# Turning branch B's queries and keys with DMA transposes instead of TensorE, in a streaming encoder step on one Trainium2 core

## The chip, the cores and the metric

The kernel runs on one core of one Trainium2 chip. The metric is the device time of one execution in microseconds (us); the time of the kernel before is the median of three runs. Beside the runs there is one profiled execution, from which every row of the trace comes.

## What is computed

One layer of a streaming encoder. A prompt of 2048 tokens and eight running streams of 16 new tokens each go through the same weights. The layer is normalised and modulated, projected by one wide matrix, mixed by two attention branches side by side, gated, merged and projected back. Cut to what matters here:

```python
h, gate = adaln_modulate(x, c, norm_g, w_ada, b_ada)
qa, ka, va, za, qb, kb, vb, zb, ga, gb = project_inputs(h, w_in, pos)   # d_model 1024

# branch A: 4 heads of 2 x 64, two softmaxes, one subtracted from the other
s = einsum('bqhcd,bkhcd->bhcqk', qa, ka) * 64 ** -0.5
p = softmax(where(mask, s, -inf)); w = p[:, :, 0] - lam * p[:, :, 1]
oa = einsum('bhqk,bkhe->bqhe', w, va)

# branch B: 8 heads of 64, stick breaking: a running product from the last key to the first
z = einsum('bqhd,bkhd->bhqk', qb, kb) * 64 ** -0.5
log_1m = where(mask, log_sigmoid(-z), 0)
a = where(mask, exp(log_sigmoid(z) + cumsum(log_1m, reverse=True) - log_1m), 0)
ob = einsum('bhqk,bkhd->bqhd', a, vb)

y = (sigmoid(ga) * ((rms(oa) * silu(za)) @ w_a) + sigmoid(gb) * ((ob * silu(zb)) @ w_b)) @ w_out
```

The outputs are the layer's rows and the new keys and values of both branches, all in float32.

## The kernel before

Products on TensorE are done in float16 with each number split into a high and a low half: high by high, high by low and low by high are added up. `q16` and `k16` are such pairs of halves for a tile of 128 tokens, with the tokens on the partitions. For the scores TensorE needs them turned, with the head's 64 numbers (and the two halves) on the partitions: these turned tiles are called `qst` (4 blocks of 128 x 128) and `k` (2 blocks).

**Units and tiles.** The middle of the kernel, from about 130 to about 1840 us, runs over 8 units. Even units are one head of branch A, odd units (`kind` 1) two heads of branch B. A unit has 17 tiles of 128 tokens: first the one of the eight streams (`t == NT`, kept as `sam` and stored for later), then 16 of the prompt. For every tile there are these steps:

- `project` (line 438): 24 products into PSUM bank `mm`; then ScalarE and VectorE write `pr` (float32 for the outputs), the values `vt`, the keys `k16` (line 304) and the queries `q16` (lines 472 and 473; one of two buffers `qbuf`). In odd units 24 more products (line 514) make gate columns in PSUM bank `t`, and ScalarE evacuates them (line 517, `gt`).
- `transpose_qk`: turns `k16` and `q16` into `k` and `qst`. It is put behind the sixth piece of the next tile's projection. Before the change six products with an identity matrix (lines 527 and 531) write into bank `t`, of which there is one buffer, and two copies (lines 541 and 542) take them to SBUF: ScalarE's in branch A, VectorE's in branch B.
- `scores` (lines 649 and 650): products of `qst` and `k`, in chunks of 512 keys; then in branch A a softmax on VectorE and ScalarE, in branch B two sigmoids on ScalarE, a scan on VectorE (line 626) and a product on GpSimd (line 632). The weights are split into halves (lines 582 and 583, or 299 and 304) and turned by a DMA from SBUF to SBUF (`turn`, line 590) into `wt`.
- `pv` (lines 706 to 711): products of `wt` with the values, two jobs later (`PV_LAG`).

**Order.** Projections run ahead of the scores by `LEAD` tiles at the start, and are spread evenly over the time; `interleave` mixes the pieces of projection, scores and `pv` in Python, and a scheduler that estimates when each instruction can begin then sets the final order on each engine. Between these pieces the weights of the next unit and the caches of the running streams are loaded and split. After the units come the cached attention of the eight streams, the merge and the output projection.

**Queue.** Nearly all DMAs are issued by SyncE (SP), one after another in the order of its program: `load` is `nc.sync.dma_start`, and the transposes of line 590 are `nc.sync.dma_start_transpose`. Among them are `hs` (line 415, the normalised input of a tile's projection), the stores of `pr` (lines 494, 495), `gt` (line 518) and `o` (line 700).

Of the kernel before, what the change touches and what calls it, by code (L numbers as in the profile page):

```python
# [17 lines left out]
F16 = mybir.dt.float16  # L18
# [7 lines left out]
P = 128  # L26
# [87 lines left out]
def layer_kernel(ctx: ExitStack, tc: tile.TileContext, a: dict):  # L114
    nc = tc.nc
    V, S, G, T = nc.vector, nc.scalar, nc.gpsimd, nc.tensor
# [79 lines left out]
    def bank(tag, dt=F32):  # L196
        return ps.tile([P, 512 if dt == F32 else 1024], dt, tag=tag, name=f"ps_{tag}", bufs=BANKS[tag])
# [5 lines left out]
    id16 = con.tile([P, P], F16, name="id16")  # L203
# [318 lines left out]
    def transpose_qk(U, t):  # L522
        g, i = t // 4, t % 4
        q16, k16 = U.pop(("q16", t)), U.pop(("k16", t))
        pt = bank("t", F16)
        for c in range(2):
            T.transpose(pt[:, c * P : (c + 1) * P], k16[:, c, :, :].rearrange("p f d -> p (f d)"), id16)
        for f in range(2):
            for c in range(2):
                j = 2 + f * 2 + c  # L530
                T.transpose(pt[:, j * P : (j + 1) * P], q16[:, f, c, :, :].rearrange("p r d -> p (r d)"), id16)
        if t == NT:
            sam = stg.tile([P, 6, P], F16, tag="sam", name="sam", bufs=1)
            qst, kst = sam[:, 0:4, :], sam[:, 4:6, :]
        else:
            if i == 0:
                U["k"][g] = kvp.tile([P, 2, 512], F16, tag="k", name="k", bufs=K_BUFS)
            U["q", t] = qst = stg.tile([P, 4, P], F16, tag="qst", name="qst", bufs=Q_BUFS)
            kst = U["k"][g][:, :, i * P : (i + 1) * P]
        copy = V.tensor_copy if U["kind"] == 1 else S.copy  # L540
        copy(out=kst, in_=pt[:, 0:256].rearrange("p (c n) -> p c n", c=2))
        copy(out=qst, in_=pt[:, 256:768].rearrange("p (j n) -> p j n", j=4))  # L542
        if t == NT:
            load(out=s_d[U["u"]][:, 0:6, :], in_=sam)

# [374 lines left out]
    for m in range(len(steps)):  # L920
        starts.append(len(line))
        for i, fn in enumerate(projection(m)):
            line.append((m, fn))
            if i == TR_AFTER and m > 0:
                line.append((m - 1, lambda m=m: transpose_qk(units[steps[m - 1][0]], steps[m - 1][1])))
    line.append((len(steps) - 1, lambda: transpose_qk(units[7], NT - 1)))
    starts.append(len(line))
    at = [0]
# [27 lines left out]
    with tc.tile_pool(name="p0", bufs=1) as p0:  # L956
# [34 lines left out]
        pt = bank("t")  # L991
# [33 lines left out]
        pt = bank("t")  # L1025
# [266 lines left out]
    for n in range(len(steps) + PV_LAG):  # L1292
        made, qk, vs = [], [], []
        if n < len(steps):
            u, t = steps[n]
# [184 lines left out]
```

## Time and profile before

| | |
|---|---|
| runs of the kernel before | 2333.37, 2330.89, 2333.27 us; median 2333.27 us |
| the profiled execution | 2326.12 us, of which the span of its instructions is 2324.3 us |
| mean granted TensorE clock | 0.969 |
| HBM read, written | 228.82 MB, 86.02 MB |

The span is the time from the first to the last instruction. A row of the busy table gives an engine's busy time, its share of the span and its count of instructions; PE is TensorE's products and PEld its weight loads. A busy time of PE is not work at its peak: products are pipelined, and each record holds its whole way through the array. DMA share is the mean busy share of the core's 16 DMA engines.

### The profile page before, as it was taken

How to read it: one execution, taken by the hardware profiler on the slowest of the kernel's cores; microseconds unless marked ns; L12 is line 12 of the kernel's file. 1: busy time of each engine (PE TensorE's matmuls, PEld its weight loads, DVE VectorE, ACT ScalarE, POOL GpSimd, SP SyncE). 2: the span in 40 equal slices, each digit the busy share in tenths (PEclk: the TensorE clock that was granted, in tenths of full speed). 3: DMA queues.
4: the chain of work that ended last, by engine and by line, in shares of the span. 5: the costliest groups of instructions: out<-in, count | busy, mean ns of one | idle time of the engine just before them, and what ended most of it. 6: DMA issues, size and time to landing. Idle time of an engine off the chain costs nothing. (4 is left out here: it accounts for less than half of the span.)

```text
span 2324.3 us, 41797 instructions
## 1 busy us (share of the span) xinstructions
PE 2096.5 (90%) x14752; PEld 1123.2 (48%) x14752; DVE 1745.0 (75%) x3795; ACT 1621.7 (70%) x3228; POOL 704.5 (30%) x610
## 2 busy tenths in 40 slices
PE   5998899998989889899998998999998689899998
PEld 3654454444545445455554444555454344444443
DVE  4658668789776777997767879787778878777763
ACT  4968676788776677878676887776677666556541
POOL 1223014356410433752023346401345312122111
PEclk7999999999999999999999999999999799999999
DMA  9778558889696798878877898665667899778421
GB/s 335 272 213 212 134 146 220 198 198 184 174 239 150 201 231 186 187 184 220 183 200 206 182 221 199 171 156 138 142 157 165 191 273 256 211 219 215 143 100 52
DMA packets 805827, 445.30 MB, mean 192 GB/s; under 512 B 537354, under 2 KB 744506, under 8 KB 805104
## 3 DMA queue, kind: packets, MB, share of 16 engines
q1 hardware_dynamic: 804668, 442.24, 76.4%
q8 instruction: 115, 1.88, 0.3%
q14 instruction: 96, 0.79, 0.1%
q10 hardware_dynamic: 948, 0.39, 0.1%
HBM read 228.82 MB, written 86.02 MB: 135 GB/s over the span
## 5 line engine op out<-in xcount | busy, mean ns | idle before, releaser
L632 POOL TENSOR_TENSOR sc_p<-sc_p,sc_n 128x127 f32<-128x127 f32 (+7 forms) x192 | 311.8, 1628 | 660.2 <-DVE sc_n L626 562.8
L438 PEld LDWEIGHTS <-hs 128*128 128x128 f16 x3120 | 276.5, 99 | 263.3 <-issue 11.9
L438 PE MATMUL ps_mm<-wa,hs 128*128 128x512 f16 x1590 | 400.4, 382 | 2.9 <-DMA hs<-hT_d 2.1
L438 PE MATMUL ps_mm<-wb,hs 128*128 128x512 f16 x1530 | 394.5, 384 | 7.6 <-DMA hs<-hT_d 6.8
L626 DVE TENSOR_TENSOR_SCAN sc_n<-ps_s,sc_n,zero_t 128x512 f32<-128x512 f32 x192 | 245.4, 1278 | 72.2 <-ACT ps_s L123 67.3
L649 PE MATMUL ps_s<-k,qst 128*128 128x512 f16 (+3 forms) x640 | 226.0, 354 | 49.2 <-DVE sc_n L626 38.5
L583 DVE TENSOR_TENSOR sc_n<-sc_p,sc_n 128x128 f16<-128x128 f32 (+7 forms) x192 | 222.7, 1163 | 36.8 <-ACT sc_n L582 36.4
L514 PEld LDWEIGHTS <-hs 128*128 128x128 f16 x1632 | 156.5, 98 | 189.1 <-ACT qst L542 5.9
L123 ACT ACTIVATE sc_p<-ps_s,usc 128x512 f32<-128x512 f32 (+3 forms) x320 | 205.1, 641 | 32.5 <-PE ps_s L650 23.3
L650 PE MATMUL ps_s<-k,qst 128*128 128x512 f16 (+3 forms) x640 | 225.7, 354 | 0.0
L514 PE MATMUL ps_t<-wb,hs 128*128 128x512 f16 x918 | 216.1, 379 | 3.0 <-DVE sam L542 1.4
L710 PE MATMUL ps_o<-v,wt 128*128 128x128 f16 x1088 | 168.9, 225 | 43.1 <-DMA wt<-sc_n 42.7
L123 ACT ACTIVATE ps_s<-ps_s,usc 128x512 f32<-128x512 f32 (+3 forms) x328 | 200.5, 611 | 0.0
L582 ACT CAST sc_n<-sc_p 128x128 f16<-128x128 f32 (+7 forms) x192 | 155.2, 811 | 63.7 <-POOL sc_p L632 62.8
L1395 PE MATMUL ps_o<-wo,wb 128*128 128x512 f16 x816 | 185.2, 382 | 6.3 <-ACT wo L299 5.5
L514 PE MATMUL ps_t<-wa,hs 128*128 128x512 f16 x714 | 170.6, 381 | 6.9 <-ACT qst L542 5.7
L710 PEld LDWEIGHTS <-wt 128*128 128x128 f16 x1088 | 105.0, 101 | 104.7 <-DMA wt<-sc_n 54.6
L711 PE MATMUL ps_o<-v,wt 128*128 128x64 f16 x1088 | 154.5, 198 | 0.0
L568 DVE TENSOR_SCALAR_CACHE_REDUCE sc_n<-ps_s,usc 128x512 f32<-128x512 f32 (+3 forms) x160 | 106.2, 664 | 35.2 <-PE ps_s L650 17.2
L1366 PEld LDWEIGHTS <-wb 128*128 128x128 f16 x816 | 79.2, 100 | 105.5 <-issue 23.1
L711 PEld LDWEIGHTS <-wt 128*128 128x128 f16 x1088 | 102.9, 100 | 50.9 <-issue 2.2
L1395 PEld LDWEIGHTS <-wb 128*128 128x128 f16 x816 | 78.7, 98 | 100.4 <-issue 9.1
(370 smaller groups left out, 4515.6 us busy)
## 6 DMA issues: line engine op xcount, KB each, us to landing
hs<-hT_d SPq DMA_DIRECT2D x130, 512.0 KB, 4.6
g_d<-gt SPq DMA_DIRECT2D x68, 256.0 KB, 4.3
out_dram<-pr SPq DMA_DIRECT2D x204, 64.0 KB, 2.2
wa<-g_d SPq DMA_DIRECT2D x25, 512.0 KB, 3.8
o_d<-o SPq DMA_DIRECT2D x136, 64.0 KB, 2.6
hs<-o_d SPq DMA_DIRECT2D x17, 512.0 KB, 3.8
out_dram<-x SPq DMA_DIRECT2D x17, 512.0 KB, 2.8
wide<-in_w_ada_dram SPq DMA_DIRECT2D x8, 1024.0 KB
```

What stands on the lines that cost most here:

```text
L123: i = S.activation(**kw)
L438: T.matmul(box["p"], box["h"][:, hi, k, :], U["w"][k][:, wi, :], start=(n == 0), stop=(n == 3 * KT - 1))
L514: T.matmul(box["g"][:, 0:gw], box["h"][:, hi, k, :], U["wg"][k // per][:, k % per, wi, :], start=(j == 0), stop=(j == 3 * KT - 1))
L582: S.copy(out=hi, in_=src)
L583: V.tensor_tensor(out=lo, in0=src, in1=hi, op=ALU.subtract)
L626: V.tensor_tensor_scan(out=dst[:, lo : lo + n][:, ::-1], data0=src[:, 0:n][:, ::-1], data1=zero_t[:, 0:1].to_broadcast([P, n]), initial=fi ...
L632: G.tensor_tensor(out=p[:, 0:m], in0=p[:, 0:m], in1=n[:, 1 : m + 1], op=ALU.mult)
L649: T.matmul(p[:, 0:n], qst[:, c, :], kk[:, c, 0:n], start=True, stop=False)
L650: T.matmul(p[:, 0:n], qst[:, 2 + c, :], kk[:, c, 0:n], start=False, stop=not diag)
L710: T.matmul(po[:, c * P : (c + 1) * P], wt[:, wj, :], vt[:, c, :, :], start=first, stop=False)
L711: T.matmul(po[:, c * P : c * P + 64], wt[:, nb + wj, :], vt[:, c, 0, :], start=False, stop=last)
L1395: T.matmul(po, st["y"][:, yi * 8 + k, :], wo[j * 4 + k // 2][:, wi, k % 2, :], start=(n == 0), stop=(n == 3 * KT - 1))
```

## The change

In branch B (`kind` 1) `transpose_qk` turns the halves with two DMA transposes from SBUF to SBUF, issued by SP: `k16` (128 x 256) into the tile's columns of `k`, and `q16` (128 x 512) into `qst`, or both into `sam` for the tile of the streams. The six products and VectorE's two copies are then not there, and the gate products have bank `t` for themselves between the transposes of branch A. Branch A keeps its products and its copies on ScalarE. The place of the step in the order written in Python is the same; the scheduler orders the engines anew.

```diff
     def transpose_qk(U, t):
         g, i = t // 4, t % 4
         q16, k16 = U.pop(("q16", t)), U.pop(("k16", t))
-        pt = bank("t", F16)
-        for c in range(2):
-            T.transpose(pt[:, c * P : (c + 1) * P], k16[:, c, :, :].rearrange("p f d -> p (f d)"), id16)
-        for f in range(2):
-            for c in range(2):
-                j = 2 + f * 2 + c
-                T.transpose(pt[:, j * P : (j + 1) * P], q16[:, f, c, :, :].rearrange("p r d -> p (r d)"), id16)
...
-        copy = V.tensor_copy if U["kind"] == 1 else S.copy
-        copy(out=kst, in_=pt[:, 0:256].rearrange("p (c n) -> p c n", c=2))
-        copy(out=qst, in_=pt[:, 256:768].rearrange("p (j n) -> p j n", j=4))
+        if U["kind"] == 1:
+            turned_to = nc.sync.dma_start_transpose
+            turned_to(out=kst, in_=k16.rearrange("p c f d -> p (c f d)"))
+            turned_to(out=qst, in_=q16.rearrange("p f c r d -> p (f c r d)"))
+        else:
+            pt = bank("t", F16)
...
```

The `else` branch holds the removed lines as they were.

More of the change, by code (lines that the diff above doesn't have):

```diff
@@ L539, in transpose_qk @@
             kst = U["k"][g][:, :, i * P : (i + 1) * P]
-        copy = V.tensor_copy if U["kind"] == 1 else S.copy
-        copy(out=kst, in_=pt[:, 0:256].rearrange("p (c n) -> p c n", c=2))
-        copy(out=qst, in_=pt[:, 256:768].rearrange("p (j n) -> p j n", j=4))
+        if U["kind"] == 1:
[4 more added lines that the diff above has]
+            pt = bank("t", F16)
+            for c in range(2):
+                T.transpose(pt[:, c * P : (c + 1) * P], k16[:, c, :, :].rearrange("p f d -> p (f d)"), id16)
+            for f in range(2):
+                for c in range(2):
+                    j = 2 + f * 2 + c
+                    T.transpose(pt[:, j * P : (j + 1) * P], q16[:, f, c, :, :].rearrange("p r d -> p (r d)"), id16)
+            copy = V.tensor_copy if U["kind"] == 1 else S.copy
+            copy(out=kst, in_=pt[:, 0:256].rearrange("p (c n) -> p c n", c=2))
+            copy(out=qst, in_=pt[:, 256:768].rearrange("p (j n) -> p j n", j=4))
         if t == NT:
```

## The prediction

> **What bounds the kernel now.** I read the page's busy table first, then busy time by unit windows, then TensorE's waits inside one branch-B unit, then one tile in the timeline, and last the DMA queue of SyncE (SP), which the change loads.
>
> ```profile
> span 2324.3 us, 41797 instructions
> PE 2096.5 (90%) x14752; PEld 1123.2 (48%) x14752; DVE 1745.0 (75%) x3795; ACT 1621.7 (70%) x3228; POOL 704.5 (30%) x610
> ```
>
> The windows below run from the first score of a unit to that of the next. Units 0 to 7 alternate between branch A (even) and branch B (odd); the first row is unit 2, the others are units 3, 5 and 7.
>
> ```profile
> core 0: us, PE busy (x) PEld busy (x) DVE busy (x) ACT busy (x) POOL busy (x), PEclk, DMA share, GB/s
> 530.00:744.00 214.00, 199.33 (x1455) 110.27 (x1455) 170.75 (x429) 160.72 (x353) 65.75 (x62) 0.98 0.81 188
> 744.00:966.00 222.00, 200.61 (x1346) 105.17 (x1345) 169.63 (x290) 168.30 (x349) 94.12 (x75) 0.98 0.85 202
> 1173.00:1398.00 225.00, 202.46 (x1370) 106.51 (x1369) 173.44 (x292) 171.57 (x358) 92.21 (x75) 0.98 0.86 203
> 1600.00:1837.00 237.00, 205.84 (x1501) 113.70 (x1499) 187.71 (x300) 174.25 (x342) 96.28 (x69) 0.92 0.69 155
> ```
>
> TensorE (PE) is busy for about 90% of a branch-B unit; VectorE and ScalarE stand at 76%, and the DMA engines at 85% in the middle units. So TensorE bounds the kernel, but by a margin of 21 us in 222, and those 21 us are waits of a microsecond or two. TensorE's waits in unit 3 (us in total, times, longest):
>
> ```profile
> PE ps_s L649 <- DVE sc_n L626: 9.2, 12, 1.7
> PE ps_o L710 <- DMA wt<-sc_n: 6.7, 4, 3.3
> PE ps_mm L438 <- DMA hs<-hT_d: 2.1, 2, 1.4
> PE ps_t L527 <- DVE k L304: 1.7, 2, 1.2
> PE ps_t L527 <- ACT gt L517: 1.3, 1, 1.3
> PE ps_t L514 <- DVE qst L542: 1.0, 1, 1.0
> ```
>
> The largest is for scans on VectorE, the next for transposes by DMA that exist already (`wt`, line 590). The last three belong to the products that the change removes and to PSUM bank `t`, which they share with the gate products of line 514.
>
> **What is removed.** One tile of unit 3 in the timeline (start us, us), with the groups of the whole run behind it (count, busy us, mean ns, idle before):
>
> ```profile
> 806.33 0.28 PE L527 MATMUL ps_t<-id,k 128*128 128x128 f16 x2
> 806.44 0.39 PE L531 MATMUL ps_t<-id,qbuf 128*128 128x128 f16 x4
> 806.92 0.81 PE L438 MATMUL ps_mm<-wb,hs 128*128 128x512 f16 x3
> 808.48 4.06 PE L438 MATMUL ps_mm<-wa,hs 128*128 128x512 f16 x18 [0.75 <-DMA hs<-hT_d]
> 813.92 0.34 DVE L304 SCALAR_TENSOR_TENSOR k<-ps_mm,usc,k 128x128 f16<-128x128 f32 x1
> 818.03 0.33 DVE L473 SCALAR_TENSOR_TENSOR qbuf<-ps_mm,usc,qbuf 128x128 f16<-128x128 f32 x1
> 835.09 0.28 DVE L541 COPY k<-ps_t 128x256 f16<-128x256 f16 x1
> 835.29 0.41 DVE L542 COPY qst<-ps_t 128x512 f16<-128x512 f16 x1
> 838.34 0.22 PE L649 MATMUL ps_s<-k,qst 128*128 128x128 f16 x1
> ...
> L531 PE MATMUL ps_t<-id,qbuf 128*128 128x128 f16 x544 | 54.8, 222 | 0.0
> L438 PE MATMUL ps_mm<-wa,hs 128*128 128x512 f16 x1590 | 400.4, 382 | 2.9 <-DMA hs<-hT_d 2.1 <-DVE v L304 0.8
> L541 DVE COPY k<-ps_t 128x256 f16<-128x256 f16 x64 | 17.7, 276 | 5.8 <-PE ps_t L531 5.7
> L542 DVE COPY qst<-ps_t 128x512 f16<-128x512 f16 x64 | 26.4, 413 | 0.0
> ```
>
> A product's 222 ns is its way through a pipeline, not its price: four end 0.39 us after the first begins, so they follow each other by (0.39 - 0.22) / 3 = 0.056 us. Branch B has 4 units of 17 tiles (16 of the prompt, one of the samples) with 6 products each: 408 x 0.056 = 23 us of TensorE. TensorE is the bound and it is in order, so I count all 23.
>
> The waits around bank `t` in unit 3 are 1.7 + 1.3 + 1.0 = 4 us, 16 over four units. The first, for `k16`, can come back as a wait of another product on the same chain of work, so I take half, 8 us, with 0 and 16 as its ends.
>
> VectorE loses 68 x (0.276 + 0.413) = 47 us, that is 47 of the 702 us that it is busy in four such units (170, 173 and 188 in the rows, 171 taken for unit 1). It isn't the bound; but TensorE waits 9.2 us a unit for its scans, 37 in all. If these shrink as VectorE's load does, 7% of 37 is 3 us; the ends are 0 and all 37. I take 3, since the wait depends on one scan after another more than on the sum of the load. Together 23 + 8 + 3 = 34 us gained.
>
> **What is added to SP.** Two transposes a tile, 136 in all, go into the queue of SP. It issues nearly every load and store of this kernel, in program order. The rows are line 590's and two lines of plain transfers in unit 3 (issue time in ns: min/median/max), then who waited, the time from issue to landing, and the DMA packets of that window:
>
> ```profile
> L590 SPq DMA_TRANSPOSE wt<-sc_n x43: 1186/1645/5289, 747.4 to 964.1; - x43
>   PEld L710: 8.4, 8
>   PE ps_o L710: 6.7, 4
> DMA to landing us min/median/max: 3.3/4.9/6.4
> L415 SPq DMA_DIRECT2D hs<-hT_d x15: 325/392/992, 759.5 to 962.7; - x15
> L495 SPq DMA_DIRECT2D out_dram<-pr x15: 382/423/577, 757.1 to 963.2; - x15
> DMA packets 91823, 44.84 MB, mean 202 GB/s; under 512 B 61221, under 2 KB 86689, under 8 KB 91802
> q1 hardware_dynamic: 91802, 44.58, 84.8%
> ```
>
> A transpose holds SP for 1.2 us at the least and 1.6 at the median, four times a plain issue. By medians SP is now busy for 43 x 1.645 = 71 us with transposes and about 111 x 0.42 = 47 us with plain issues (111 are listed in this window; the two rows are typical): 118 of 222. The change adds 34 x 1.2 to 34 x 1.645, 41 to 56 us a unit, which brings SP to 72 to 78% by medians, and nearer to full with the 5 us issues that the maximum shows. SP also stops for each new transpose until `k16` or `q16` is written. Queued behind it then are the `wt` transposes that TensorE's lines 710 and 711 wait for, the `hs` loads of line 438, and the stores that free `pr`, `gt` and `o`.
>
> The DMA engines get 13,056 rows of 256 B a unit, 3.3 MB. By bytes that is 3.3 / 44.6 of 188 us (84.8% of 222), 14 us; by packets, if each row is one, 13,056 / 91,802 of it, 27 us. Their share goes from 85% to between 91 and 97%, so landings get later too.
>
> The price at TensorE: 12 of 43 `wt` transposes ended a wait there. If 28% of the added issue time reaches it, that is 0.28 x 136 x 1.645 = 63 us. The lower end is 0, as the instruction lists of the two built programs show: from a head's last score to its first product of line 710, TensorE has 13 us of other products before and 18 after in tile 6 of unit 3, and 15 and 27 in tile 8. The later `wt` tolerate a slower SP; those of tiles 0 to 3 don't (12, 9 and 13 us before; 14, 9 and 11 to 13 after). I take 30 us, half-way.
>
> Here a rule of the Trainium skill speaks. "DMA: Bandwidth & Descriptors", section "Issuing engines are not separate DMA queues", says that a sequencer's time to initiate a DMA is usually small relative to the DMA itself. In this trace it is 1.6 of 4.9 us for a transpose, a third, so the trace differs; by the rule this term would be near nothing, and the sum that of the first rival.
>
> **What is moved.** Before, the first score of tile 8 (838.34) follows the copies (835.70) by 2.6 us, and these come 17 us after `q16` was ready (818.36): the six products stand behind the gate products in bank `t`. Without that tie the lists put the scores earlier. A 512-column product costs (4.06 - 0.38) / 17 = 0.216 us; weighted so by columns, the products between the end of a tile's projection and its first score come to 27 us before and 15 after in tile 8 of unit 3, 29 and 17 in tile 9, 32 and 18 in tile 10; units 1 and 5 are within 4 us of that, and in unit 7 tiles 6 to 10 stand at 13 to 18 after. That makes 14 tiles with at most 19 us. The new chain in tile 8: projection ends at 807.73, `q16` is ready 10.6 us later, then about 1 us until SP is free, and 4.9 us to landing: 16.5 us. With 15 to 19 us of products over 90% busy, 17 to 21 us, some scores wait and others don't. I take 1.3 us for each of 14, 18 us; the ends are 0 and 14 x 5 = 70 (a whole landing each).
>
> **Sum.** -34 + 30 + 18 = +14 us. On the profiled execution (2326.12 us, 1.8 around its span) that gives 2340; the median of the runs shown lies 7.15 higher, so the forecast is 2347 us, 0.6% slower.
>
> **Rivals.** First, faster: the added issues fall into SP's idle time, and with line 710 standing later half of its 6.7 us a unit goes too (13 us). Then 34 + 13 - 18 - 4 (what is left of SP's price) = 25 us gained, 2308. For it: SP waits for nearly half the window, and bank `t` is free. Against it: that idle time is in-order waiting for others, which added work doesn't fill neatly. This is what the skill's rule above would give.
>
> Second, much slower: SP becomes a bound beside TensorE. It decides once a late transpose delays TensorE, whose delay then delays the inputs of the next transposes. With the upper 63 us of the SP price and 2 us at each of the 14 scores (28), less 34, it gives +57, 2390. For it: issues of 5.3 us and a DMA share of over 90%. Against it: the slack that the new order gives to tiles 4 to 15.
>
> Third, no change: gain and price within 5 us of each other, 2333.
>
> **How the numbers follow.** 0.2% is about what a measurement of this kernel can tell from no change. The forecast gets 0.40, the much slower case 0.14, no change 0.09, the faster case 0.37: slower 0.54, the same 0.09, faster 0.37. Cases of both signs hold much of the chance. The forecast's own range is 2338 to 2375 (SP's price between 21 and 58 us). The range over all goes from the faster case with 5 us more, 2303, to the much slower one with 5 us more, 2395; a fifth is left for a gain of all 16 us at bank `t` or more of the 37 us of scan waits, and for scores that wait a whole landing.
>
> **What would show it.** Right: TensorE's lines for branch B's transposes are gone, and busy PE is about 90 us lower (408 x 0.22, as records overlap), with the span no shorter; line 649 waits for DMAs into `qst` or `k`, some 18 us; the waits of line 710 and 438 for DMAs are larger by 30; DMA share in units 3 and 5 over 0.90; the new issues take 1.2 to 1.7 us. Wrong: a shorter span, with no waits of line 649 for DMAs and fewer of line 710; or SP's issues growing to 3 us and more, and waits for DMAs above 100 us in all.

## The result and the profile after

| | before | after |
|---|---|---|
| median of the runs | 2333.32 us (2330.89 to 2334.67, 4 runs) | 2349.18 us (2347.93 to 2352.28, 4 runs) |
| profiled execution, span | 2326.12, 2324.3 us | 2349.34, 2347.4 us |

The changed kernel takes 1.0071 times as long, with a 95% interval of 1.0054 to 1.0089: about 16 us slower, where 14 us (2347) was forecast. Size and sign came as forecast. The parts of the sum did not all do so, and one part was missing.

The busy table and the DMA queue after the change:

```profile
span 2347.4 us, 41282 instructions
PE 2094.5 (89%) x14344; PEld 1109.5 (47%) x14344; DVE 1706.4 (73%) x3659; ACT 1619.4 (69%) x3228; POOL 706.3 (30%) x610
q1 hardware_dynamic: 861244, 455.63, 79.9%
```

408 products are gone (14752 to 14344), VectorE is busy for 39 us less, and the DMA queue carries 13.4 MB more. Yet TensorE is busy for only 2 us less, and its idle time, the span less its busy time, grew from 227.8 to 252.9 us. The windows in units 3 and 5 are as long as the ones shown before the change, and start 8 and 17 us later, as the units now do:

```profile
core 0: us, PE busy (x) PEld busy (x) DVE busy (x) ACT busy (x) POOL busy (x), PEclk, DMA share, GB/s
752.00:974.00 222.00, 200.52 (x1282) 102.70 (x1280) 161.97 (x263) 169.25 (x355) 94.88 (x73) 0.96 0.90 209
1190.00:1415.00 225.00, 197.47 (x1267) 101.18 (x1265) 158.95 (x260) 169.58 (x355) 90.85 (x73) 0.96 0.91 209
```

DMA share rose from 0.85 and 0.86 to 0.90 and 0.91, about the lower end of the 0.91 to 0.97 that was forecast. PEclk, the granted clock of TensorE, fell from 0.98 to 0.96 in both, which was not forecast. Now TensorE's waits over the whole run, first before, then after (us in total, times, longest):

```profile
PE ps_o L710 <- DMA wt<-sc_n: 42.7, 29, 4.9
PE ps_s L649 <- DVE sc_n L626: 38.5, 45, 3.4
PE ps_o L706 <- DMA wt<-sc_n: 20.8, 19, 2.6
PE ps_t L527 <- DVE k L304: 9.0, 8, 2.0
PE ps_mm L438 <- DMA hs<-hT_d: 9.0, 5, 3.0
PE ps_t L527 <- ACT gt L517: 3.6, 5, 1.3
```

```profile
PE ps_o L715 <- DMA wt<-sc_n: 50.4, 29, 4.9
PE ps_s L654 <- DVE sc_n L631: 48.9, 51, 2.4
PE ps_o L711 <- DMA wt<-sc_n: 25.6, 19, 4.5
PE ps_mm L438 <- DMA hs<-hT_d: 8.4, 2, 5.0
PE ps_s L654 <- DMA qst<-qbuf: 5.6, 4, 3.3
PE ps_t L540 <- DVE k L304: 4.7, 3, 2.1
```

Waits for `wt` grew by 12 us, for scans by 10, and the new wait for `qst` is 5.6 us; the waits at bank `t` shrank by 8 in these rows. Most rows of such a list change whenever the order does, as the runs below show, so one row is not a price by itself. The new issues of SP (min/median/max in ns) and their landings:

```profile
L535 SPq DMA_TRANSPOSE k<-k x64: 1167/1172/2097, 252.4 to 1789.7; - x64
L536 SPq DMA_TRANSPOSE qst<-qbuf x64: 1188/1217/2125, 258.1 to 1791.0; - x64
DMA to landing us min/median/max: 2.4/2.5/3.8
```

One place shows all parts at once. It is SP's timeline of the changed kernel, then TensorE's in the same microseconds (start us, us), and then three windows with the granted clock:

```profile
845.07 8.16 SPq L595 DMA_TRANSPOSE wt<-sc_n  x2
853.32 0.53 SPq L705 DMA_DIRECT2D o_d<-o  x1
853.96 1.17 SPq L595 DMA_TRANSPOSE wt<-sc_n  x1
855.22 0.53 SPq L518 DMA_DIRECT2D g_d<-gt  x1
855.80 1.18 SPq L535 DMA_TRANSPOSE k<-k  x1
857.07 1.22 SPq L536 DMA_TRANSPOSE qst<-qbuf  x1
```

```profile
855.68 0.59 PE L514 MATMUL ps_t<-wa,hs 128*128 128x512 f16 x2
859.55 0.39 PE L654 MATMUL ps_s<-k,qst 128*128 128x256 f16 x1 [3.27 <-DMA qst<-qbuf]
...
860.23 0.61 PE L654 MATMUL ps_s<-k,qst 128*128 128x512 f16 x1
860.64 0.63 PE L655 MATMUL ps_s<-k,qst 128*128 128x512 f16 x1
861.07 1.06 PE L514 MATMUL ps_t<-wa,hs 128*128 128x512 f16 x2
...
864.64 0.38 PE L654 MATMUL ps_s<-k,qst 128*128 128x512 f16 x1
864.85 0.38 PE L655 MATMUL ps_s<-k,qst 128*128 128x512 f16 x1
```

```profile
core 0: us, PE busy (x) PEld busy (x) DVE busy (x) ACT busy (x) POOL busy (x), PEclk, DMA share, GB/s
856.30:859.10 2.80, 0.00 (x0) 0.00 (x0) 2.41 (x6) 1.73 (x7) 1.30 (x1) 1.00 0.59 158
859.20:862.50 3.30, 2.95 (x12) 1.46 (x13) 0.35 (x1) 0.19 (x1) 1.01 (x2) 0.50 0.85 222
862.60:866.00 3.40, 3.40 (x22) 1.64 (x21) 0.00 (x0) 1.60 (x4) 0.00 (x0) 1.00 1.15 257
```

SP's issues follow each other without a pause from 845 on, two `wt` transposes taking 8.16 us of it; the queries' transpose gets its turn at 857.07 and lands 2.5 us later. TensorE stands still for 3.27 us. After that, products of 512 columns follow each other by 0.41 to 0.43 us until about 862.5, and by 0.21 again at 864; the granted clock is 0.50 from 859.2 to 862.5 and 1.00 in the windows on both sides. So here a wait of three microseconds is followed by another three at half speed. The Trainium skill's page "TensorE: Matmul & The Clock Gate" states in its section "Part 1: The HAM clock gate" that the array's clock goes to half after an idle window of about 3.4 us and back to full after a busy one. The trace agrees with the halving and the return; the wait here, 3.27 us, is a little shorter than that window. The mean clock bounds what this costs: in 13 timed runs of the kernel before it was 0.967 to 0.970, in the four of the changed kernel 0.958 to 0.962. Of 2349 us, 0.008 is 18 us, and this is an upper bound, since TensorE also idles in part of the slow time.

### The profile page after: what moved, and what is told of

Read it like the earlier page. It is cut to its first block, busy times and chain, and to the rows that moved or that the text cites. A ratio compares the mean times of both kernels' runs of the same rounds, so it can differ in the third digit from the quotient of the medians.

```text
span 2347.4 us, 41282 instructions
## 1 busy us (share of the span) xinstructions
PE 2094.5 (89%) x14344; PEld 1109.5 (47%) x14344; DVE 1706.4 (73%) x3659; ACT 1619.4 (69%) x3228; POOL 706.3 (30%) x610
## 5 line engine op out<-in xcount | busy, mean ns | idle before, releaser
L637 POOL TENSOR_TENSOR sc_p<-sc_p,sc_n 128x127 f32<-128x127 f32 (+7 forms) x192 | 319.2, 1666 | 528.4 <-DVE sc_n L631 506.2
L438 PEld LDWEIGHTS <-hs 128*128 128x128 f16 x3120 | 276.0, 99 | 261.6 <-issue 9.7
L654 PE MATMUL ps_s<-k,qst 128*128 128x512 f16 (+3 forms) x640 | 228.1, 357 | 70.6 <-DVE sc_n L631 48.9
L588 DVE TENSOR_TENSOR sc_n<-sc_p,sc_n 128x128 f16<-128x128 f32 (+7 forms) x192 | 211.6, 1106 | 42.5 <-ACT sc_n L587 42.1
L715 PE MATMUL ps_o<-v,wt 128*128 128x128 f16 x1088 | 192.7, 227 | 50.5 <-DMA wt<-sc_n 50.4
L514 PE MATMUL ps_t<-wb,hs 128*128 128x512 f16 x918 | 235.4, 385 | 0.0
L514 PEld LDWEIGHTS <-hs 128*128 128x128 f16 x1632 | 145.3, 99 | 142.7 <-issue 11.7
L514 PE MATMUL ps_t<-wa,hs 128*128 128x512 f16 x714 | 183.4, 387 | 6.0 <-ACT qst L547 6.0
L716 PE MATMUL ps_o<-v,wt 128*128 128x64 f16 x1088 | 173.7, 199 | 0.0
L715 PEld LDWEIGHTS <-wt 128*128 128x128 f16 x1088 | 108.1, 103 | 137.3 <-DMA wt<-sc_n 62.7
L716 PEld LDWEIGHTS <-wt 128*128 128x128 f16 x1088 | 106.2, 101 | 72.6 <-issue 3.5
L573 DVE TENSOR_SCALAR_CACHE_REDUCE sc_p<-ps_s,usc 128x512 f32<-128x512 f32 (+3 forms) x160 | 106.5, 666 | 43.9 <-PE ps_s L655 27.2
L631 DVE TENSOR_TENSOR_SCAN sc_n<-ps_s,zero_t 128x128 f32<-128x128 f32 (+3 forms) x128 | 104.1, 815 | 41.1 <-ACT ps_s L123 40.2
```

The source lines that it names most:

```text
L438: T.matmul(box["p"], box["h"][:, hi, k, :], U["w"][k][:, wi, :], start=(n == 0), stop=(n == 3 * KT - 1))
L514: T.matmul(box["g"][:, 0:gw], box["h"][:, hi, k, :], U["wg"][k // per][:, k % per, wi, :], start=(j == 0), stop=(j == 3 * KT - 1))
L573: V.tensor_scalar(out=dst[:, lo : lo + n], in0=p[:, 0:n], scalar1=sc_pos, scalar2=None, op0=ALU.mult, op1=ALU.max, accum_out=job["mx"][:, ...
L588: V.tensor_tensor(out=lo, in0=src, in1=hi, op=ALU.subtract)
L631: V.tensor_tensor_scan(out=dst[:, lo : lo + n][:, ::-1], data0=src[:, 0:n][:, ::-1], data1=zero_t[:, 0:1].to_broadcast([P, n]), initial=fi ...
L637: G.tensor_tensor(out=p[:, 0:m], in0=p[:, 0:m], in1=n[:, 1 : m + 1], op=ALU.mult)
```

## The experiments

Two theories were left. **SP's queue**: the added issues hold up in-order SP, and TensorE waits for what is queued behind. **The order**: the scheduler's order before is a good one, and any other is slower. A third, **the packets**, puts the price on the DMA engines. Every ratio is to the kernel before, run on the same chip, with its 95% interval.

**The gain without the price.**

```diff
-            turned_to(out=kst, in_=k16.rearrange("p c f d -> p (c f d)"))
-            turned_to(out=qst, in_=q16.rearrange("p f c r d -> p (f c r d)"))
+            V.tensor_copy(out=kst, in_=k16.rearrange("p c f d -> p c (f d)"))
+            V.tensor_copy(out=qst, in_=q16.rearrange("p f c r d -> p (f c) (r d)"))
```

> The change with its two transposes left out: VectorE copies k16 and q16 unturned from SBUF to k and qst, so branch B's scores are of unturned halves. This has the gain without the price. The prediction's sum (23 us of products, 8 at bank t, scans hardly helped because VectorE's copies stay) says 2333 - 31 = 2302 us, 2300 to 2312. A rival, that the time hangs on the order which the scheduler happens to find and not on the work removed, says 2325 to 2350.

Measured: 2315.73 us, 0.9931 [0.9912, 0.9949], 16 us gained instead of 31; this misses both expectations, and is nearer to the sum than to the rival. The profile of this run:

```profile
span 2316.3 us, 40981 instructions
PE 2084.5 (90%) x14344; PEld 1107.0 (48%) x14344; DVE 1756.0 (76%) x3795; ACT 1620.4 (70%) x3228; POOL 710.7 (31%) x610
PE ps_s L653 <- DVE sc_n L630: 50.2, 55, 3.7
```

Busy TensorE is 12 us less than before where 23 us of products went, so slower products took some 11 us back: the four timed runs have a clock of 0.961 to 0.965, where the kernel before has about 0.968, and 0.005 of 2316 us is 12 us at most. Its idle time did not fall but rose by 4 us (231.8 against 227.8): the waits for scans grew from 38.5 to 50.2 us, which undoes the 8 us foreseen at bank `t`. No transfer was added here, so the lower clock comes with less work on TensorE, or with the new order, and not with SP.

**The price without the gain.**

```diff
         copy(out=qst, in_=pt[:, 256:768].rearrange("p (j n) -> p j n", j=4))
+        if U["kind"] == 1:
+            beside = stg.tile([P, 6, P], F16, tag="sam", name="sam", bufs=1) if t < NT else None
+            if beside is not None:
+                nc.sync.dma_start_transpose(out=beside[:, 0:2, :], in_=k16...)
+                nc.sync.dma_start_transpose(out=beside[:, 2:6, :], in_=q16...)
```

> The kernel before, and beside its products and copies the two DMA transposes of each prompt tile of branch B into a tile that nobody reads (128 transposes). This has the price at SP and at the DMA engines without the gain and without any score waiting for them. The prediction's price of 30 us says 2363 us, its upper end of 63 us 2396. If the price comes mostly from scores that wait for the turned queries, or from the new order, 2333 to 2343.

Measured: 2353.36 us, 1.0101 [1.0067, 1.0135], some 23 us by the ratio (16 to 31 by its interval), between the two expectations and nearer to the price of 30. Gain and price measured apart add up to +7; the change is at +16. The profile of this run has the price in another place than the prediction:

```profile
span 2349.2 us, 42179 instructions
PE 2114.9 (90%) x14752; PEld 1132.4 (48%) x14752; DVE 1732.3 (74%) x3795; ACT 1624.9 (69%) x3228; POOL 703.3 (30%) x610
PE ps_o L715 <- DMA wt<-sc_n: 56.2, 34, 5.5
PE ps_s L654 <- DVE sc_n L631: 28.2, 33, 3.4
PE ps_o L711 <- DMA wt<-sc_n: 18.1, 18, 2.8
```

The same 14752 products keep TensorE busy for 18 us longer than before, at a mean clock of 0.961 instead of 0.969, and its idle time grew by only 6.5 us (234.3 against 227.8). Waits for `wt` grew by 11 us, and waits for scans fell by 10.

**Issues or packets.** The first of these keeps the issues and cuts the packets to a third; the second keeps the packets and makes the issues plain ones.

```diff
+            nc.sync.dma_start_transpose(out=beside[:, 0:1, :], in_=k16[:, 0, :, :]...)
+            nc.sync.dma_start_transpose(out=beside[:, 2:3, :], in_=q16[:, 0, 0, :, :]...)
```

> As the run with both transposes beside the kept products, but each of the two transposes turns one block of 128 x 128 alone: the same 128 issues of about 1.2 us on SP, a third of the packets (256 rows a tile instead of 768). If the issues on SP carry the price, it stays at about 2333 + 22, 2348 to 2358 us. If the packets carry it, 2335 to 2343. If it is the scheduler's order alone, it may lie anywhere from 2330 to 2350.

```diff
+    beside_d = dram.tile([P, 6, 2 * P], F16, name="beside_d")
...
+            load(out=beside_d[:, 0:2, 0:P], in_=k16.rearrange("p c f d -> p c (f d)"))
+            load(out=beside_d[:, 2:6, 0:P], in_=q16.rearrange("p f c r d -> p (f c) (r d)"))
```

> The kernel before, and beside its products two plain transfers of k16 and q16 a prompt tile of branch B into a spare place in HBM, laid out so that each row of 256 B is a packet of its own: the packets of the two transposes (768 a tile), but plain issues of 0.4 us on SP. If SP's issue time carries the price, a third of 22 us, 2335 to 2343 us. If the packets carry it, 2350 to 2358.

The issue times, of the small transposes first, then of the plain transfers:

```profile
L545 SPq DMA_TRANSPOSE sam<-k x64: 1099/1127/1896, 274.2 to 1791.4; - x64
L546 SPq DMA_TRANSPOSE sam<-qbuf x64: 1107/1177/2517, 275.4 to 1792.6; - x64
```

```profile
L545 SPq DMA_DIRECT2D beside_d<-k x64: 367/407/1649, 247.0 to 1782.4; - x64
L546 SPq DMA_DIRECT2D beside_d<-qbuf x64: 366/424/1628, 272.9 to 1783.3; - x64
```

TensorE's waits for `wt`, in the same order:

```profile
PE ps_o L714 <- DMA wt<-sc_n: 51.9, 32, 4.8
PE ps_o L710 <- DMA wt<-sc_n: 15.2, 17, 1.9
```

```profile
PE ps_o L714 <- DMA wt<-sc_n: 56.4, 43, 4.9
PE ps_o L710 <- DMA wt<-sc_n: 19.4, 19, 2.0
```

Measured: small transposes 2353.34 us, 1.0085 [1.0057, 1.0114]; plain transfers 2341.45 us, 1.0033 [1.0013, 1.0053]. With about a third of the packets the price is still 20 us by the ratio, and with nearly all of them but a third of the issue time it falls to 8. That speaks for the issues on SP and against the packets. It is not shown beyond doubt. In each of these kernels the scheduler put the same 14752 products of TensorE in a sequence that is neither that of the kernel before nor that of the other two. The price does not grow evenly with the issues: when TensorE begins its 6000th product (967.8 us in the kernel before, near the end of the second of the four units of branch B), the run with the full transposes is 5 us behind and that with the small ones 6.5, of 25 and 24 at the end. Nor does the route by `wt` follow the price: the waits for `wt` are 67 us with the small transposes and 76 with the plain transfers, against 63.5 before, the smaller rise with the higher price. The rule of the Trainium skill that the prediction weighed ("DMA: Bandwidth & Descriptors", section "Issuing engines are not separate DMA queues": the time to initiate a DMA is usually small relative to the DMA itself) does not hold for these transposes: 1.1 to 1.2 us of a landing of 2.3 to 2.5 us is the issue.

**The order by itself.**

```diff
-LEAD = 5.0
+LEAD = 5.1
```

> The kernel before with LEAD 5.1 in place of 5.0: the same work in a slightly different order. If the order as such is worth little, 2333 us within 5. If the result of the change is the scheduler's luck, this moves by 10 us or more either way.

Measured: 2338.12 us, 1.0038 [1.002, 1.0056]: 6 us by the medians, 9 by the ratio, between the two expectations. A change that moves only the order costs as much as the plain transfers did. What is left of a price under 10 us can therefore not be told from a change of order.

**Half of the change.** The keys go through TensorE and VectorE as before:

```diff
-            turned_to(out=kst, in_=k16.rearrange("p c f d -> p (c f d)"))
+            pt = bank("t", F16)
+            for c in range(2):
+                T.transpose(pt[:, c * P : (c + 1) * P], k16[:, c, :, :].rearrange("p f d -> p (f d)"), id16)
+            V.tensor_copy(out=kst, in_=pt[:, 0:256].rearrange("p (c n) -> p c n", c=2))
```

> The change for the queries alone; the keys keep their two products and VectorE's copy. Half of the added issues, two thirds of the added packets, two thirds of the products gone. If gain and price both scale, it lies between the two kernels, 2338 to 2346 us. If the wait for turned queries (the later of the two) is what costs, it is as slow as the change, 2347 to 2352.

Measured: 2344.93 us, 1.0053 [1.0034, 1.0072], between the two kernels, as scaling says; with these intervals it decides little.

**SP relieved.** Three ways, each in both kernels. First, four stores issued by GpSimd:

```diff
-            load(out=out_rows(nk, t, h * P, P), in_=rot[:, 128:256])
+            G.dma_start(out=out_rows(nk, t, h * P, P), in_=rot[:, 128:256])
```

(and so for the values, `o` and `gt`).

> The changed kernel with the stores of new keys and values, of o and of gt (lines 494, 495, 518 and 700 of the kernel before) issued by GpSimd instead of SP: some 340 issues of 0.4 us off SP, the same bytes through the DMA engines. If SP's queue carries the price of the change, 2349 goes down to 2320 to 2338 us. If the load on the DMA engines carries it, 2345 to 2355. GpSimd's issues may cost its own work time, which would show in its lines.

> The kernel before with the same four stores issued by GpSimd, the control for that run of the changed kernel (2345 us). If stores from GpSimd cost nothing by themselves, 2328 to 2336 us, and taking 154 us of issues off SP won the changed kernel only 4 us. If they cost something, 2340 or more, and SP's relief was worth that much more.

Second, 240 stores left out:

```diff
+            if t == 0 or t == NT:
-            load(out=out_rows(nk, t, h * P, P), in_=rot[:, 128:256])
+                load(out=out_rows(nk, t, h * P, P), in_=rot[:, 128:256])
```

(and so for the values).

> The changed kernel with the stores of new keys and values left out for tiles 1 to 15 of every unit: 240 plain issues of 0.4 us fewer on SP, and no other engine does anything instead (those outputs stay unwritten). To be read against the same omission in the kernel before. If SP's queue carries the price, the change is no longer 17 us slower than its counterpart but between 16 us faster (the gain measured without transposes) and 5 us slower. If the price is the scheduler's order or the DMA engines, it stays 12 to 22 us slower.

> The counterpart: the kernel before with the same 240 stores left out. SP was not full there, so little is won: 2315 to 2331 us.

Third, two of the stores issued by ScalarE:

```diff
-            load(out=out_rows(nv, t, h * P, P), in_=pr[:, 256:384])
+            S.dma_start(out=out_rows(nv, t, h * P, P), in_=pr[:, 256:384])
```

(and so for `gt`).

> The changed kernel with the stores of new values and of gt (lines 495 and 518 of the kernel before), whose data ScalarE has just written, issued by ScalarE instead of SP: 204 issues fewer on SP, nothing left out. If SP carries the price and ScalarE (69% busy) can take 204 issues, 2325 to 2343 us, and if it comes under 2331 it beats both kernels. If ScalarE's own queue then delays the sigmoids, 2350 or more.

> The counterpart: the kernel before with the same 204 stores issued by ScalarE. Little to win at SP, something to lose on ScalarE: 2325 to 2345 us. If SP carries the price of the change, the changed kernel with these stores is less than 17 us slower than this one, or faster.

| SP's queue | kernel before so altered | changed kernel so altered | difference |
|---|---|---|---|
| as it was | 2333.32 us | 2349.18 us, 1.0071 | +16 |
| 240 stores left out | 2344.99 us, 1.0057 [1.0037, 1.0076] | 2336.38 us, 1.0030 [1.0012, 1.0047] | -9 |
| two stores on ScalarE | 2343.41 us, 1.0048 [1.0029, 1.0067] | 2339.48 us, 1.0034 [1.0016, 1.0052] | -4 |
| four stores on GpSimd | 2380.24 us, 1.0195 [1.0166, 1.0225] | 2345.40 us, 1.0062 [1.0041, 1.0082] | -35 |

By the ratios, each to the kernel before on the same chip, the three differences are -6, -3 and -31 us, and that of the stores on ScalarE lies within the intervals. In all three the change is no longer dearer than its counterpart, which is what SP's queue predicts. But about half of each shift or more comes from the counterparts, which got slower, even the one that only leaves work out: 12 us where 2 to 18 us of gain was expected. Its order is new as well, which is the likeliest reason, but was not tested.

The order theory fits much of this too. Three kernels that should cost next to nothing (LEAD 5.1, 240 stores less, two stores on ScalarE) came at 2338 to 2345 us, and the relieved versions of the change at 2336 to 2345. Above this level stand the change at 2349 and the two kernels with transposes beside the products at 2353. If any new order brings a kernel to that level, SP's issues explain 8 to 15 us of the 20 to 23 there, by this estimate.

The four stores are 476 issues (GpSimd has 1086 instructions with them and 610 without), not the 340 of the expectation. For the changed kernel alone, 2345 us was what that expectation gave to the load on the DMA engines; the control gave it another reading, since GpSimd adds a cost of its own: an issue there takes 0.56 us and stands in line with its products.

```profile
L700 POOL DMA_DIRECT2D o_d<-o x136 | 76.2, 560 | 175.9 <-ACT o L685 120.2 <-ACT junk L281 35.8 <-ACT k L299 7.9
L518 POOL DMA_DIRECT2D g_d<-gt x68 | 38.2, 561 | 285.1 <-ACT gt L517 276.1 <-ACT o L685 5.5 <-ACT sc_p L123 2.2
```

This is the kernel before with its stores there: GpSimd idles for 285 and 176 us ahead of these issues, until ScalarE has written the data, and its other work stands behind them. No complete version came under the kernel before.

## Why the prediction was right, point by point

**TensorE's products, 23 us, with bank `t`, 8, and scans, 3.** The work went and bank `t`'s waits fell, but measured without transposes the gain is 16 us, not the 31 foreseen for it. The step that failed is "I count all 23": busy TensorE fell by 12 us only, with a lower clock. The scans' term had the wrong sign: those waits rose from 38.5 to 48.9 us in the changed kernel, and to 50.2 without transposes.

**SP's price, 30 us.** Measured beside the kept products it is 23, within its ends of 0 and 63, and the runs point to the issues, as the prediction argued, with some part of it due to the new order. Its route was wrong there: 6.5 us came as idle time of TensorE and 18 as slower products, at a clock of 0.959 to 0.964 in the timed runs. In the change itself the listed waits for `wt` grew by 12 us, and lines 710 and 438, where 30 was to be seen, by 7 together. The upper end rests on a double count: the 4 waits of products for `wt` and the 8 of weight loads are not 12 transposes, since a product and its weight load wait for the same one (at 766.8, 771.1 and 787.9 us of the kernel before). With 8 of 43 the upper end is 42 us and half-way 21, and the forecast would have been 2338. Why the clock falls when the idle time hardly grows stays open.

**Scores that wait for queries, 18 us.** Mis-sized: 5.6 us in four waits. The chain used the median landing of all transposes, 4.9 us, while these small ones land in 2.5; the shortest landing in the same row, 3.3, was nearer.

**What was missing.** The clock. The span grew by 23.1 us: TensorE's idle time by 25.1, while its busy time fell by 2.0 although 23 us of products are gone, so slower products put back some 21. The listed parts add up to the same: 23 us of products less; waits for `wt`, scans and `qst` 28 more and at bank `t` 8 less; and a mean clock of 0.958 instead of 0.969, which over these spans is 99 - 72 = 27 us of lost full-speed time, an upper bound since part of it is idle. That gives at most +24. The waits came out at 28 - 8 = 20 us instead of the 30 + 18 - 8 - 3 = 37 foreseen, and the clock, which had no term, filled the gap. So the forecast of +14 came near the measured +16 by luck in good part: two errors met.

**The sign to look for "busy PE about 90 us lower"** was a wrong reading: it multiplied records that overlap. One after another the products come to 23 us, and slower products put about as much back: busy time fell by 2 us.

**Other signs and readings.** Waits for DMAs above 100 us were named, together with SP issues of 3 us and more, as a sign that the forecast is wrong. They came to 107 us, but had been 90 before, so this threshold told little, and the new issues stayed at 1.2 us. The windows said to end at the next unit's first score end earlier: unit 3's scans run from 749 to 991 us, its window from 744 to 966. The waits per unit are therefore somewhat low, and their sum of 37 us for the scans is near the 38.5 of the whole run all the same.

**The rivals.** The faster case asked for room on SP, and with SP relieved the change is 3 to 31 us cheaper than its counterpart by the ratios, though the counterparts had become slower themselves; on the real queue it is not cheaper. No change and the much slower case did not come.

**Open.** Gain and price measured apart give +7, the change +16. The other 9 are no more than the intervals of the three measurements allow together, about 10, and as large as what a new order alone cost (6 to 12 us); they include the waits for `qst`. These runs don't tell such things apart, and so leave open how the price of 20 to 23 us divides between SP's issues and the order. Nor was it tried to hold the order fixed while the instructions change.

## What to carry to other kernels

Moving work from the bounding engine to a DMA frees that engine's cycles but spends the issuing queue's: price the issue (here 1.2 us, three times a plain one) on the in-order queue, and name what stands behind it. Where the bounding engine's clock falls after a wait, as it did here to 0.50 for 3.3 us after a wait of 3.27, count such a wait about one and a half times: half of the slow 3.3 us are lost too. Compare idle time and busy time of the bounding engine before and after, since a slower clock shows in its busy time and in no list of waits. In a kernel whose order has been tuned, measure a neutral reordering too before a difference of half a per cent is put down to a cause.

## What the runs showed of the hardware

The small transposes' cost barely depends on their size: issue medians of 1.13 and 1.18 us for one block of 128 x 128, 1.17 for two and 1.22 for four; landings of 2.3 to 2.9 us at the median. And TensorE's speed can halve after a short wait even in a kernel that is 90% busy: after a wait of 3.27 us the granted clock was 0.50 for 3.3 us, with up to 0.43 us between products of 512 columns, against 0.21 three microseconds later.
